# The output projection's second half in a hybrid encoder block: weight parts prepared two tiles ahead on VectorE, the norm spread over the tiles, the first MLP parts cast earlier

## The chip, the cores and the metric

The kernel runs on one core of one Trainium2 chip, as one launch. The metric is device time in microseconds (us), lower is better; a kernel's time is the median of its runs.

## The reference

One encoder layer over 1024 tokens of width 1024, in float32. Cut to what matters here:

```python
def rmsnorm(x, g):
    y = xf * lax.rsqrt(jnp.mean(xf * xf, axis=-1, keepdims=True) + EPS)
    return y * g

def hybrid_mixer(h, ...):
    proj = rmsnorm(h, ln_g) @ w_in          # 1024 x 3104
    ...                                     # 2-D neighbourhood attention (8 heads x 64), gated linear attention (4 heads)
    return jnp.concatenate([y_na, y_gla], axis=-1) @ w_out      # 1024 x 1024

def sqrelu_mlp(h, ln_g, w1, w2):            # w1: 1024 x 4096, w2: 4096 x 1024
    return jnp.square(jax.nn.relu(rmsnorm(h, ln_g) @ w1)) @ w2

h = h + hybrid_mixer(h, ...)
h = h + sqrelu_mlp(h, ...)
out = rmsnorm(h, ln_final_g)
```

## The kernel before

Everything is held transposed: the feature dimension lies on the 128 partitions, the 1024 tokens along the free dimension, in two halves of 512 (`hf` 0 and 1). `hT` is the residual stream, eight tiles `d` of 128 features.

Each float32 operand of a large product is split into two fp32r parts: a high part, which ScalarE makes by a cast (`S.copy`), and a low part, the difference, made by VectorE or GpSimd (POOL in the profile). A product is three matmuls: high times high, high times low, low times high. So every weight tile costs one cast and one subtraction before TensorE can finish with it.

A list scheduler puts the instructions of each engine in a fixed order by priority. Within an engine they then run strictly in that order. `tc.keep_in_program_order` pins an instruction to its place in the program's text among the others pinned so; all of TensorE's instructions are pinned, and so is nearly everything in the MLP (`kp`). `tc.high_priority` moves code ahead.

The part around the change, in order of time:

- Output projection, second half. `sums(1, d, KO, ...)` is 24 matmuls of 128x512 into a PSUM bank `op1_d`, for `d` = 0 to 7; `add` then adds the bank to `hT` on VectorE. Its weights come from `weights(w_out[d], eng)`: a load `wf` (queue of SP), a cast `wh` on ScalarE and one 128x1024 subtraction `wl`, on VectorE for `d` below 4 and on GpSimd from 4 on. `wf`, `wh` and `wl` have two buffers each in the pool `stg`.
- `opl_d` are eight short products that finish the first half of the tokens (the last block of the concatenated heads came late).
- `ff_in(hf, d)` squares `hT[:, d]` on ScalarE (`sq`) and adds it up in `acc0` (GpSimd) or `acc1` (VectorE); `ff_sum(hf)` sums over partitions with a matmul by ones (`v2_0`, `v2_1`), and `rstd_from` makes the reciprocal root from it (`r0`, `r1`) in four ScalarE and two VectorE instructions.
- After tile 2, `r0` is made, and for all eight `k` the normed tile `nf` (VectorE), its cast (ScalarE) and its low part (VectorE): `n0`, the MLP's input for the first half of the tokens.
- The MLP. `First`/`FirstPlain` stages compute `w1` products, `Second`/`SecondPlain` the `w2` ones; four chunks of `w1`/`w2` of 512 KB tiles `A11`, `A12`, `A21`, `A22`. The first chunk is plain: a `FirstPlain` stage of 16 half-steps of 12 matmuls (`u<-...` in the profile; `ph` and `pl` are the high and low part of the weight piece), the first eight for the first half of the tokens (input `n0`), the last eight for the second half (inputs `T4` and `B22`). Then 16 half-steps of `SecondPlain` (`f<-...`).
- Before the `FirstPlain` stage starts, the `ph` and `pl` of its first two half-steps are made (`to_two`); after the first half-step comes `ff_sum(1)`, then `r1`. The normed tiles of the second half (`normed`, `b` in the profile, then a cast and a low part into `T4` or `B22`), and later the sums for a Strassen-like scheme (`sums123`, with GpSimd's `whole`), are given out over the half-steps as `job`s.

`prepare(k)` issues, ahead of half-step `k`, the casts and low parts for half-step `k+2`, the activations of `k-1` and then the jobs.

Of the kernel before, what the change touches and what calls it, by code (L numbers as in the profile page):

```python
# [10 lines left out]
F32 = mybir.dt.float32  # L11
F32R = mybir.dt.float32r
U32 = mybir.dt.uint32
AF = mybir.ActivationFunctionType
ALU = mybir.AluOpType
# [3 lines left out]
P = 128  # L19
D = 1024  # L20
T = 1024
H = 512
NK = D // P
# [43 lines left out]
def block_kernel(ctx, tc, xT, g_mix, w_in, w_z, rpb, na_mask, gu, gb, g_gla, sel_f, sel_b,  # L67
                 rst, w_out, g_ff, w1, w2, g_fin, out):
    nc = tc.nc
    V, S, DMA, G = nc.vector, nc.scalar, nc.sync, nc.gpsimd  # L70

    L = "left"
    R = "right"
    pool = lambda name, side, bufs=1: tc.tile_pool(name=name, bufs=bufs, side=side)
# [7 lines left out]
    stg = stg_stack.enter_context(pool("stg", L, 2))  # L82
# [40 lines left out]
    class Fill:  # L123
# [24 lines left out]
        def run(self, steps=1 << 30):  # L148
            while steps > 0 and self.gens:
                steps -= self.step()  # L150
# [84 lines left out]
    yg_pool = ctx.enter_context(ExitStack())  # L235
# [456 lines left out]
    def to_parts(hf, ks, eng):  # L692
        c = slice(hf * H, (hf + 1) * H)
        t = yhl[hf]
        for k in ks:
            i = KO.index(k)
            S.copy(t[:, i, 0, :], yk(k)[:, c])
            (eng if i % 2 else V).tensor_tensor(t[:, i, 1, :], yk(k)[:, c], t[:, i, 0, :].bitcast(F32), op=ALU.subtract)  # L698
# [5 lines left out]
    def sums(hf, d, ks, eng=None, w=None, ahead=()):  # L704

        w = w or weights(w_out[d], eng)
        o = bank("mm", f"op{hf}_{d}")
        for i, _ in enumerate(out_mm(o, hf, w, ks)):
            to_parts(hf, ahead[i:i + 1], G)
            yield  # L710
        add(hf, d, o)
# [207 lines left out]

    a2 = ctx.enter_context(pool("a2", R))  # L920
    a3 = yg_pool.enter_context(pool("a3", L))
    yp_stack = ExitStack()
    yp = yp_stack.enter_context(pool("op", R, 2))
    n0, acc = half(a2, "n0"), {}

    def ff_in(hf, d):
        c = slice(hf * H, (hf + 1) * H)
        if d == 0:
            acc[hf] = sq = yp.tile([P, H], F32, tag="acc", name=f"acc{hf}")
        else:  # L930
            sq = yp.tile([P, H], F32, tag="sq", name="sq2")
        S.activation(sq, hT[:, d, c], AF.Square)
        if d:
            (V if hf else G).tensor_tensor(acc[hf], acc[hf], sq, op=ALU.add)

# [9 lines left out]
    def to_two(h, l, x, eng=None, kept=False):  # L945

        c = S.copy(h, x)  # L947
        if kept:
            tc.keep_in_program_order(c)
        (eng or V).tensor_tensor(l, x, h.bitcast(F32), op=ALU.subtract)  # L950
# [10 lines left out]
    wk = split(wf, G)  # L961
    to_parts(0, KO[-1:], V)
    to_parts(1, KO, V)
    run(sums(1, 0, KO, w=w10))
    for d in range(NK):
        o = bank(("t", "s", "o")[d % 3], f"opl_{d}")
        t = yhl[0][:, NK - 1]
        run(product(o, wk, lambda k: t[:, 0, :], lambda k: t[:, 1, :], ks=(0,), woff=d * P))
        add(0, d, o)
        ff_in(0, d)  # L970
    ff_in(1, 0)
    for d in range(1, NK):
        run(sums(1, d, KO, V if d < 4 else G))
        ff_in(1, d)
        if d == 2:
            r0 = rstd_from(ff_sum(0), 1.0 / D, yp, "rs", H, "sq", 2, y=acc[0])
            for k in range(NK):
                nf = yp.tile([P, H], F32, tag="nf", name="nf")
                normed_h(nf, 0, k, r0)
                to_two(n0[:, k, 0, :], n0[:, k, 1, :], nf)  # L980
# [215 lines left out]
    class FirstPlain(Stage):  # L1196
# [9 lines left out]
        def mm(self, p, kh):  # L1206
            (hf, m), w = p, self.parts.pop((p, kh))
            if kh == 0:
                self.o = bank("s" if hf else "mm", f"u{hf}_{m}")
            t, k0 = npt[f"B{kh + 1}{hf + 1}"]  # L1210
            for k in range(4):
                for n, (a, x) in enumerate(((w[0], 0), (w[0], 1), (w[1], 0))):
                    PE.matmul(self.o, a[:, k * P:(k + 1) * P], t[:, k0 + k, x, :],
                              start=kh == k == n == 0, stop=kh == 1 and k == 3 and n == 2)
            if kh:
                self.last = self.o
# [59 lines left out]
    def go_on(n):  # L1276
        for _ in range(n):
            k = at[0]
            st, p, i = halves[k]
            prepare(k)  # L1280
            lows = []
            if k + 1 < len(halves) and halves[k + 1][0].gated and halves[k + 1][2] == 0:
                lows = [(halves[n][0], halves[n][1:]) for n in (k + 1, k + 2)]
            if st.gated:
                st.mm(p, i, lows)
            else:
                for t, q in lows:
                    t.lows(*q)
                st.mm(p, i)
            at[0] += 1  # L1290


    f1 = FirstPlain(0)
    stage(f1)
    with tc.high_priority(offset=150):
        for n in range(2):
            p, i = f1.order[n]
            ph = mp.tile([P, H], F32R, tag="ph", name="ph", bufs=3)
            pl = mp.tile([P, H], F32R, tag="pl", name="pl", bufs=3)
            to_two(ph, pl, f1.w.t[f"A{p[1] // 2 + 1}{i + 1}"][:, 0:H])  # L1300
            f1.parts[p, i] = ph, pl
    go_on(1)
    v1 = ff_sum(1)
    r1 = ub("r1")
# [234 lines left out]
```

## Time and profile before

| | |
|---|---|
| median of 3 runs | 1193.68 us (1193.57 to 1195.28) |
| the profiled execution | 1193.91 us, of which the span from first to last instruction is 1192.1 us |
| mean granted TensorE clock | 0.99 |
| busy: TensorE, VectorE, ScalarE, GpSimd | 97%, 73%, 56%, 21% |
| output projection, second half (`op1_1` to `op1_7`) | 493.4 to 537.7 us of the span |
| first MLP stages (`FirstPlain`, `SecondPlain`) | from 539.8 us |

Times in rows of the trace are us from the start of the span. In a timeline row stand the start, the duration, the engine, the source line, the operation, the tile written and the tiles read, the number of merged instructions, and in brackets how long the engine was idle before it and what released it. TensorE's matmuls overlap: a 128x512 one lasts 0.39 us, but the next starts 0.23 us after it, so lost time is read from the distance of starts. A line of the code can be that of a helper: all matmuls are L114, and L1012 and L950 are low parts.

### The profile page before, as it was taken

The page shows a single profiled execution, that of the slowest core. Times are in us where ns is not written, and L with a number is a line of the kernel's source. Part 1 is how long each engine was busy: PE and PEld are TensorE (multiplying, and loading weights), DVE is VectorE, ACT ScalarE, POOL GpSimd, SP SyncE. Part 2 cuts the span into 40 slices and gives each one's busy share as a digit, 9 for nine tenths or more (in the row PEclk, how much of TensorE's full clock was granted, in tenths as well). Part 3 has the DMA queues.
Part 4 walks back from the last instruction along what each step waited for, and adds up shares of the span by engine and source line. Part 5 has one row for each costly group of instructions (what it writes and reads, how often), then busy time and mean ns, then how long its engine had stood idle before and what let it go on. Part 6 is the DMA issues. An engine that isn't in the chain of part 4 may idle for free.

```text
span 1192.1 us, 15428 instructions
## 1 busy us (share of the span) xinstructions
PE 1154.5 (97%) x5632; PEld 945.5 (79%) x5632; DVE 865.0 (73%) x1554; ACT 665.0 (56%) x1222; POOL 248.9 (21%) x203
## 2 busy tenths in 40 slices
PE   8999999989999999999999999999999999999996
PEld 8878778767787878877688888888888888888876
DVE  8777867856767786585858885877859768597455
ACT  6867566556666665435634635545455454453664
POOL 4200000202011124530103230411404114032005
PEclk9999999999999999999999999999999999999999
DMA  7333132322313252330210121111211121111203
GB/s 238 74 87 92 42 73 56 77 65 54 80 42 100 67 177 71 106 106 1 71 66 21 56 71 62 37 54 62 71 53 36 54 71 55 53 53 53 71 1 142
DMA packets 40283, 84.03 MB, mean 70 GB/s; under 512 B 9264, under 2 KB 20656, under 8 KB 40208
## 3 DMA queue, kind: packets, MB, share of 16 engines
q1 hardware_dynamic: 36608, 71.11, 17.8%
q0 software_dynamic: 3456, 11.94, 5.8%
q8 instruction: 44, 0.72, 0.2%
q14 instruction: 31, 0.25, 0.1%
q10 hardware_dynamic: 144, 0.00, 0.0%
HBM read 78.85 MB, written 5.96 MB: 71 GB/s over the span
## 4 chain that ended last, share of the span: by engine, by line
PE 77%; DVE 12%; ACT 6%; issue 2%; DMA 1%; POOL 0%; SPq 0%; DVEq 0%; ACTq 0%
PE f L114 26%; PE u L114 22%; PE proj L114 14%; PE op L114 5%; PE sc L114 2%; PE o L114 2%; PE no L114 2%; PE pt L119 1%; DVE st L595 1%; DVE st L592 1%; DVE pl L1012 1%; DVE asb L587 1%; DVE nf L942 1%; PE sb L114 1%; PE ob L114 1%
## 5 line engine op out<-in xcount | busy, mean ns | idle before, releaser
L1034 ACT CAST ph<-A 128x512 fp32r<-128x512 f32 x166 | 103.0, 621 | 146.4 <-PE f L114 73.6
L1012 POOL TENSOR_TENSOR ul<-uB,uh 128x512 fp32r<-128x512 f32 x84 | 109.2, 1319 | 330.4 <-ACT uh L1047 213.4
L114 PE MATMUL f<-uh,ph 128*128 128x512 f32 x400 | 155.9, 390 | 1.5 <-ACT u L1055 1.3
L114 PE MATMUL f<-ul,ph 128*128 128x512 f32 x400 | 155.7, 389 | 0.1
L114 PE MATMUL f<-uh,pl 128*128 128x512 f32 x400 | 155.7, 389 | 0.0
L1012 DVE TENSOR_TENSOR pl<-A,ph 128x512 fp32r<-128x512 f32 x166 | 112.7, 688 | 52.6 <-ACT ph L1034 52.6
L114 PE MATMUL proj<-nh,wh 128*128 128x512 f32 x352 | 150.5, 428 | 0.0
L114 PE MATMUL proj<-nh,wl 128*128 128x512 f32 x352 | 138.8, 394 | 1.2 <-DMA wl<-in_w_in 1.2
L114 PE MATMUL proj<-nl,wh 128*128 128x512 f32 x352 | 138.3, 393 | 0.0
L1194 DVE TENSOR_TENSOR hT<-hT,f 128x512 f32<-128x512 f32 x168 | 113.0, 686 | 20.0 <-PE f L114 20.0
L114 PE MATMUL u<-n,ph 128*128 128x512 f32 x288 | 90.3, 395 | 2.0 <-ACT ph L947 2.0
L114 PEld LDWEIGHTS f<-uh,ph 128*128 128x128 f32 x400 | 75.1, 188 | 17.9 <-ACT u L1055 1.8
L114 PEld LDWEIGHTS f<-ul,ph 128*128 128x128 f32 x400 | 75.1, 188 | 16.0 <-DVE ul L1012 0.4
L114 PEld LDWEIGHTS f<-uh,pl 128*128 128x128 f32 x400 | 75.1, 188 | 15.6
L114 PEld LDWEIGHTS proj<-nh,wh 128*128 128x128 f32 x352 | 66.6, 189 | 18.1 <-issue 5.6
L1047 ACT CAST uh<-uB 128x512 fp32r<-128x512 f32 x84 | 51.9, 618 | 51.0 <-PE f L114 34.2
L114 PEld LDWEIGHTS proj<-nh,wl 128*128 128x128 f32 x352 | 66.4, 189 | 16.7 <-DMA wl<-in_w_in 1.6
L114 PE MATMUL u<-T,ph 128*128 128x512 f32 x256 | 79.2, 391 | 0.1
L114 PE MATMUL op<-y,wh 128*128 128x512 f32 x240 | 76.9, 401 | 0.4 <-DVE y L698 0.4
L114 PEld LDWEIGHTS proj<-nl,wh 128*128 128x128 f32 x352 | 66.8, 190 | 11.7 <-issue 1.7
L114 PE MATMUL u<-nt,ph 128*128 128x512 f32 x224 | 69.0, 389 | 0.0
L806 ACT ACTIVATE xsc<-xsc,sm 128x384 f32<-128x384 f32 (+1 forms) x64 | 37.3, 584 | 51.4 <-DVE sm L804 51.0
(300 smaller groups left out, 2489.8 us busy)
## 6 DMA issues: line engine op xcount, KB each, us to landing
A<-in_w SPq DMA_DIRECT2D x64, 512.0 KB
wf<-in_w_in SPq DMA_DIRECT2D x22, 512.0 KB
wl<-in_w_in POOLq DMA_DIRECT2D x21, 512.0 KB, 6.8
wf<-in_w_out SPq DMA_DIRECT2D x17, 512.0 KB
hT<-in_xT SPq DMA_DIRECT2D x2, 2048.0 KB
xs<-in_xT SPq DMA_DIRECT2D x6, 512.0 KB
out<-hT SPq DMA_DIRECT2D x4, 512.0 KB
out<-hT SPq DMA_DIRECT2D x8, 256.0 KB
```

The lines of the kernel that those rows point to most:

```text
L114: m = nc.tensor.matmul(*args, **kw)
L119: tc.keep_in_program_order(nc.tensor.transpose(*args, **kw))
L587: V.copy_predicated(asb[hf], sel.bitcast(U32).to_broadcast([P, 4, P]), src.rearrange("p (a b) -> p a b", a=4))
L592: V.scalar_tensor_tensor(st[0:64, i + 1, :], st[0:64, i, :], dec[0:64, i:i + 1], st[0:64, i + 1, :], op0=ALU.mult, op1=ALU.add)
L595: V.scalar_tensor_tensor(st[64:128, j - 1, :], st[64:128, j, :], dec[64:128, j:j + 1], st[64:128, j - 1, :], op0=ALU.mult, op1=ALU.add)
L806: S.activation(x[:, :n], x[:, :n], AF.Exp, scale=-1.0, bias=sm[:, i, 0:1], accum_out=sm[:, i, 1:2])
L942: V.scalar_tensor_tensor(dst, hT[:, d, hf * H:(hf + 1) * H], gff[:, d:d + 1], r, op0=ALU.mult, op1=ALU.mult)
L1012: return kp(eng.tensor_tensor(l, x, h.bitcast(F32), op=ALU.subtract))
L1034: kp(S.copy(ph, x))
L1047: kp(S.copy(uh, x))
L1194: kp(V.tensor_tensor(hT[:, d, c], hT[:, d, c], o[:, s], op=ALU.add))
```

## The change

Four edits.

1. `out_w(d)` replaces `weights` for `d` = 1 to 7 of the second half. It is called two tiles ahead of use (`d` = 1 before `op1_0`, `d` = 2 after it, `d+2` at tile `d`). The parts live in three places: a new pool `w3` for `d` = 1, 4, 7, and the two buffers of `stg` for the others. The subtraction is always on VectorE, in two halves of 128x512, and cast and subtractions are pinned.
2. The norm of the first half of the tokens (`nf`, cast, low part) is spread: two `k` at each of the tiles 3 to 6, rather than all eight after tile 2.
3. The casts of the MLP's first two weight pieces are pinned, and `ff_in(1, 7)`, its square pinned too, now stands after them in the program.
4. `FirstPlain.mm` runs the three kinds of product in the outer loop and `k` in the inner one: four high-high, four high-low, four low-high.

```diff
@@ -919,6 +919,7 @@
 
     a2 = ctx.enter_context(pool("a2", R))
     a3 = yg_pool.enter_context(pool("a3", L))
+    w3 = yg_pool.enter_context(pool("w3", L))
     yp_stack = ExitStack()
     yp = yp_stack.enter_context(pool("op", R, 2))
     n0, acc = half(a2, "n0"), {}
@@ -929,7 +930,9 @@
             acc[hf] = sq = yp.tile([P, H], F32, tag="acc", name=f"acc{hf}")
         else:
             sq = yp.tile([P, H], F32, tag="sq", name="sq2")
-        S.activation(sq, hT[:, d, c], AF.Square)
+        q = S.activation(sq, hT[:, d, c], AF.Square)
+        if hf and d == NK - 1:
+            tc.keep_in_program_order(q)
         if d:
             (V if hf else G).tensor_tensor(acc[hf], acc[hf], sq, op=ALU.add)
 
@@ -961,7 +964,22 @@
     wk = split(wf, G)
     to_parts(0, KO[-1:], V)
     to_parts(1, KO, V)
+
+    def out_w(d):
+
+        wf = stg.tile([P, D], F32, tag="wf", name="wf")
+        DMA.dma_start(wf, w_out[d])
+        places = w3 if d % 3 == 1 else stg
+        wh = places.tile([P, D], F32R, tag="wh", name="wh")
+        wl = places.tile([P, D], F32R, tag="wl", name="wl")
+        tc.keep_in_program_order(S.copy(wh, wf))
+        for c in (slice(0, H), slice(H, D)):
+            tc.keep_in_program_order(V.tensor_tensor(wl[:, c], wf[:, c], wh[:, c].bitcast(F32), op=ALU.subtract))
+        return wh, wl
+
+    w1d = {1: out_w(1)}
     run(sums(1, 0, KO, w=w10))
+    w1d[2] = out_w(2)
     for d in range(NK):
         o = bank(("t", "s", "o")[d % 3], f"opl_{d}")
         t = yhl[0][:, NK - 1]
@@ -970,11 +988,15 @@
         ff_in(0, d)
     ff_in(1, 0)
     for d in range(1, NK):
-        run(sums(1, d, KO, V if d < 4 else G))
-        ff_in(1, d)
+        if d + 2 < NK:
+            w1d[d + 2] = out_w(d + 2)
+        run(sums(1, d, KO, w=w1d.pop(d)))
+        if d < NK - 1:
+            ff_in(1, d)
         if d == 2:
             r0 = rstd_from(ff_sum(0), 1.0 / D, yp, "rs", H, "sq", 2, y=acc[0])
-            for k in range(NK):
+        if 2 < d < NK - 1:
+            for k in (2 * d - 6, 2 * d - 5):
                 nf = yp.tile([P, H], F32, tag="nf", name="nf")
                 normed_h(nf, 0, k, r0)
                 to_two(n0[:, k, 0, :], n0[:, k, 1, :], nf)
@@ -1208,8 +1230,8 @@
             if kh == 0:
                 self.o = bank("s" if hf else "mm", f"u{hf}_{m}")
             t, k0 = npt[f"B{kh + 1}{hf + 1}"]
-            for k in range(4):
-                for n, (a, x) in enumerate(((w[0], 0), (w[0], 1), (w[1], 0))):
+            for n, (a, x) in enumerate(((w[0], 0), (w[0], 1), (w[1], 0))):
+                for k in range(4):
                     PE.matmul(self.o, a[:, k * P:(k + 1) * P], t[:, k0 + k, x, :],
                               start=kh == k == n == 0, stop=kh == 1 and k == 3 and n == 2)
             if kh:
@@ -1297,8 +1319,9 @@
             p, i = f1.order[n]
             ph = mp.tile([P, H], F32R, tag="ph", name="ph", bufs=3)
             pl = mp.tile([P, H], F32R, tag="pl", name="pl", bufs=3)
-            to_two(ph, pl, f1.w.t[f"A{p[1] // 2 + 1}{i + 1}"][:, 0:H])
+            to_two(ph, pl, f1.w.t[f"A{p[1] // 2 + 1}{i + 1}"][:, 0:H], kept=True)
             f1.parts[p, i] = ph, pl
+    ff_in(1, NK - 1)
     go_on(1)
     v1 = ff_sum(1)
     r1 = ub("r1")
```

What this does to the instruction order, at three places. First GpSimd, in the second half of the output projection: `acc0` is the sum of squares of the first half, `wl` are the low parts of tiles 4 to 7, `b11` the first of the MLP's `whole` sums. Before:

```order
L934 TENSOR_TENSOR acc0_4623<-acc0_4623,sq2_4678 128x512
L197 TENSOR_TENSOR wl_4833<-wf_4830,wh_4832 128x1024
L197 TENSOR_TENSOR wl_4868<-wf_4865,wh_4867 128x1024
L197 TENSOR_TENSOR wl_4903<-wf_4900,wh_4902 128x1024
L197 TENSOR_TENSOR wl_4938<-wf_4935,wh_4937 128x1024
L1321 TENSOR_TENSOR b11_5214<-n0_4482 128x512
L1321 TENSOR_TENSOR b11_5261<-n0_4482 128x512
```

After, the four subtractions are gone from GpSimd. VectorE has them instead; from the add of `op1_2` on it now runs (`wl_4785` belongs to tile 5, `wl_4829` to tile 6):

```order
L716 TENSOR_TENSOR hT_4112<-hT_4112,op1_2_4743 128x512
L937 TENSOR_TENSOR acc1_4698<-acc1_4698,sq2_4769 128x512
L230 TENSOR_TENSOR rst_4774<-rst_4774,rsu_4777 128x512
L231 SCALAR_TENSOR_TENSOR acc0_4640<-rst_4774,acc0_4640 128x512
L977 TENSOR_TENSOR wl_4785<-wf_4782,wh_4784 128x512 x2
L945 SCALAR_TENSOR_TENSOR nf_4818<-hT_4112,gff_82,acc0_4640 128x512
L716 TENSOR_TENSOR hT_4112<-hT_4112,op1_3_4789 128x512
L945 SCALAR_TENSOR_TENSOR nf_4822<-hT_4112,gff_82,acc0_4640 128x512
L953 TENSOR_TENSOR n0_4485<-nf_4818,n0_4485 128x512
L937 TENSOR_TENSOR acc1_4698<-acc1_4698,sq2_4815 128x512
L953 TENSOR_TENSOR n0_4485<-nf_4822,n0_4485 128x512
L977 TENSOR_TENSOR wl_4829<-wf_4826,wh_4828 128x512 x2
```

The low part of tile 5 stands before the add of tile 3, that of tile 6 before the add of tile 4, and two normed tiles lie between.

Second, ScalarE where the MLP begins: `sq2` are the squares of tiles 5 to 7, `ph` the first weight pieces. Before:

```order
L932 ACTIVATE sq2_4897<-hT_4112 128x512
L932 ACTIVATE sq2_4932<-hT_4112 128x512
L932 ACTIVATE sq2_4967<-hT_4112 128x512
L947 CAST ph_4992<-A11_4984 128x512
L947 CAST ph_4996<-A12_4986 128x512
```

After:

```order
L933 ACTIVATE sq2_4940<-hT_4112 128x512
L950 CAST ph_5000<-A11_4992 128x512
L950 CAST ph_5004<-A12_4994 128x512
L933 ACTIVATE sq2_5008<-hT_4112 128x512
L1056 CAST ph_5011<-A11_4992 128x512
```

The two casts now stand ahead of the square of tile 7, which waits for the last add. VectorE follows in the same manner; before:

```order
L716 TENSOR_TENSOR hT_4112<-hT_4112,op1_7_4941 128x512
L934 TENSOR_TENSOR acc1_4681<-acc1_4681,sq2_4967 128x512
L950 TENSOR_TENSOR pl_4993<-A11_4984,ph_4992 128x512
L950 TENSOR_TENSOR pl_4997<-A12_4986,ph_4996 128x512
L1012 TENSOR_TENSOR pl_5002<-A11_4984,ph_5000 128x512
```

After, with both `pl` between the last add and the last sum of squares:

```order
L716 TENSOR_TENSOR hT_4112<-hT_4112,op1_7_4951 128x512
L953 TENSOR_TENSOR pl_5001<-A11_4992,ph_5000 128x512
L953 TENSOR_TENSOR pl_5005<-A12_4994,ph_5004 128x512
L937 TENSOR_TENSOR acc1_4698<-acc1_4698,sq2_5008 128x512
L1034 TENSOR_TENSOR pl_5013<-A11_4992,ph_5011 128x512
```

Third, TensorE at the same place, from the first half-step of the MLP to `v2_1`. Before, high-high, high-low and low-high alternate for each `k`:

```order
L114 MATMUL u0_0_5004<-n0_4482,ph_4992 128x512 x2
L114 MATMUL u0_0_5004<-n0_4482,pl_4993 128x512
L114 MATMUL u0_0_5004<-n0_4482,ph_4992 128x512 x2
L114 MATMUL u0_0_5004<-n0_4482,pl_4993 128x512
L114 MATMUL u0_0_5004<-n0_4482,ph_4992 128x512 x2
L114 MATMUL u0_0_5004<-n0_4482,pl_4993 128x512
L114 MATMUL u0_0_5004<-n0_4482,ph_4992 128x512 x2
L114 MATMUL u0_0_5004<-n0_4482,pl_4993 128x512
L114 MATMUL v2_1_5017<-acc1_4681,ones_79 128x512
```

After:

```order
L114 MATMUL u0_0_5015<-n0_4485,ph_5000 128x512 x8
L114 MATMUL u0_0_5015<-n0_4485,pl_5001 128x512 x4
L114 MATMUL v2_1_5028<-acc1_4698,ones_79 128x512
L114 MATMUL u0_0_5015<-n0_4485,ph_5004 128x512 x8
L114 MATMUL u0_0_5015<-n0_4485,pl_5005 128x512 x4
```

The low part `pl` is first read by the ninth matmul of a half-step, not by the third; `v2_1` stays after twelve. The same loop order holds for the half-steps on `T4` and `B22`.

## The prediction

> **What bounds the kernel now.** I read the page's busy shares and chain of waits first, then TensorE's work in stretches of 20 us, then its timeline where a stretch is short of work, and last what the other engines do there.
>
> ```profile
> span 1192.1 us, 15428 instructions
> ...
> PE 1154.5 (97%) x5632; PEld 945.5 (79%) x5632; DVE 865.0 (73%) x1554; ACT 665.0 (56%) x1222; POOL 248.9 (21%) x203
> ...
> PE 77%; DVE 12%; ACT 6%; issue 2%; DMA 1%; POOL 0%; SPq 0%; DVEq 0%; ACTq 0%
> ```
>
> TensorE bounds the kernel: 97% busy, 77% of the chain. Only time in which it stands or runs slowly can be won. The stretches show where (TensorE's busy us with its matmul count come first, the granted clock is third from the end):
>
> ```profile
> 500.00:520.00 20.00, 20.00 (x88) 16.20 (x87) 16.11 (x17) 10.26 (x16) 7.15 (x4) 1.00 0.34 105
> 520.00:540.00 20.00, 15.16 (x57) 11.12 (x56) 14.70 (x17) 7.00 (x12) 7.75 (x4) 0.91 0.21 80
> 540.00:560.00 20.00, 19.91 (x78) 15.63 (x79) 10.75 (x17) 10.63 (x19) 0.00 (x0) 0.91 0.00 0
> ...
> 580.00:600.00 20.00, 17.65 (x73) 13.03 (x72) 17.00 (x26) 13.57 (x25) 1.78 (x1) 1.00 0.24 80
> 600.00:620.00 20.00, 20.00 (x90) 16.57 (x89) 12.23 (x20) 6.99 (x12) 0.00 (x0) 1.00 0.16 52
> ```
>
> A full stretch has 88 to 90 matmuls. From 520 to 560 there are 57 and 78, in tiles 5 to 7 of the projection and the MLP's start, which is where the change works. TensorE's timeline there:
>
> ```profile
> 505.80 0.62 PE L114 MATMUL op<-y,wh 128*128 128x512 f32 x2
> ...
> 521.47 0.61 PE L114 MATMUL op<-y,wh 128*128 128x512 f32 x2
> 523.11 0.50 PE L114 MATMUL op<-y,wl 128*128 128x512 f32 x1 [1.03 <-POOL wl L197]
> ...
> 528.40 0.73 PE L114 MATMUL op<-y,wh 128*128 128x512 f32 x2
> 530.92 0.75 PE L114 MATMUL op<-y,wl 128*128 128x512 f32 x1 [1.79 <-POOL wl L197]
> ...
> 534.67 0.40 PE L114 MATMUL op<-y,wl 128*128 128x512 f32 x1
> ...
> 537.42 0.39 PE L114 MATMUL op<-y,wl 128*128 128x512 f32 x1
> 539.82 0.73 PE L114 MATMUL u<-n,ph 128*128 128x512 f32 x2 [2.01 <-ACT ph L947]
> 540.64 0.50 PE L114 MATMUL u<-n,pl 128*128 128x512 f32 x1
> ...
> 544.58 1.06 PE L114 MATMUL v<-acc,ones 128*128 128x512 f32 x2
> ```
>
> From 505.80 to 521.47 start 69 matmuls: 0.227 us each. That is the measure for what follows. Two kinds of loss show: waits, and after two of them a lower clock:
>
> ```profile
> 532.00:536.00 4.00, 4.00 (x14) 3.17 (x13) 1.58 (x2) 0.63 (x1) 1.79 (x2) 0.70 0.00 0
> 540.00:544.00 4.00, 3.91 (x11) 2.81 (x12) 1.79 (x3) 0.81 (x2) 0.00 (x0) 0.65 0.00 0
> 260.00:264.00 4.00, 3.25 (x8) 1.59 (x9) 2.73 (x14) 2.20 (x7) 0.00 (x0) 0.67 0.64 176
> 596.00:600.00 4.00, 3.60 (x16) 2.98 (x17) 2.63 (x5) 2.61 (x6) 0.00 (x0) 1.00 0.41 135
> ...
> 260.37 0.44 PE L114 MATMUL sc<-k00p,q 128*128 128x384 f32 x1 [2.21 <-DVE sm L804]
> ...
> 596.39 0.50 PE L114 MATMUL f<-uh,ph 128*128 128x512 f32 x1 [1.35 <-ACT u L1055]
> ```
>
> Waits of 1.79, 2.01 and 2.21 us were followed by clocks of 0.70, 0.65 and 0.67; the wait of 1.35 was not (1.00).
>
> **The change part by part.** *Weights two tiles ahead.* In tiles 6 and 7 the low part comes late, since GpSimd needs 2.4 us for it and starts only after a cast that itself waits its turn:
>
> ```profile
> 520.67 2.38 POOL L197 TENSOR_TENSOR wl<-wf,wh 128x1024 fp32r<-128x1024 f32 x1 [4.70 <-ACT wh L196]
> 528.42 2.44 POOL L197 TENSOR_TENSOR wl<-wf,wh 128x1024 fp32r<-128x1024 f32 x1 [5.36 <-ACT wh L196]
> 530.82 2.97 POOL L1321 TENSOR_TENSOR b<-n 128x512 f32<-128x512 f32 x2
> ...
> 513.75 2.77 DVE L942 SCALAR_TENSOR_TENSOR nf<-hT,gff,acc 128x512 f32<-128x512 f32 x1
> ...
> 516.44 0.68 DVE L950 TENSOR_TENSOR n<-nf,n 128x512 fp32r<-128x512 f32 x1
> 517.04 0.68 DVE L934 TENSOR_TENSOR acc<-acc,sq 128x512 f32<-128x512 f32 x1
> ...
> 518.25 1.40 DVE L942 SCALAR_TENSOR_TENSOR nf<-hT,gff,acc 128x512 f32<-128x512 f32 x2
> ...
> 516.38 85.84 SPq L1021 DMA_DIRECT2D A<-in_w  x10
> ```
>
> Lost in tile 6: 523.11 less 521.47 less two starts (0.45) is 1.2, and 0.1 in the next starts. Tile 7: 530.92 less 528.40 less 0.45 is 2.1, 0.2 ahead of it, and the slow clock from 530.92 to 534.67, nine matmuls in 3.75 instead of 2.04, is 1.7. Together 5.3, of which 1.7 is the clock's.
>
> Does it all go? VectorE now carries per tile two half subtractions, two `nf`, two low parts, an add and a sum of squares. Its starts lie 0.60 apart (516.44, 517.04), 0.70 for `nf` (two in 1.40): 6 x 0.60 + 2 x 0.70 = 5.0 us against a tile's 24 x 0.227 = 5.45. It is nearly full, but the 128x1024 subtraction on GpSimd also goes, beside which one `nf` took 2.77 instead of 0.70; that is 2 us back per tile. Two of GpSimd's `whole` sums stay (2.97 for both). Walking down the two orders with these durations, tile 6's low part is done near 516 for a need at 521, tile 7's near 521 (523 with both `whole` sums in its way) for a need at 526.5. With margins of 3.5 to 5 us I take all 5.3.
>
> Both ends of that: if no two VectorE instructions overlapped (8 x 0.69 = 5.5 per tile, 0.1 over the tile's 5.45) and both `whole` sums stood fully in its way (3.0), it would be 3.3 us late after four tiles, of which the 3.0 are in the 523 already: no loss in the weights. So the cost lies between 0 and what that lag does at the MLP's start, below. A gain beyond 5.3 is excluded, since the waits and the slow stretch are all there is to win here.
>
> The loads: SP issued `A11` at 516.38, behind tile 7's weights, which waited for GpSimd's low part of tile 5. Now that is VectorE's, right behind `r0`, near 511; the MLP's pieces come no later. Cost 0.
>
> *Norm spread.* The same 24 instructions, off TensorE's path; they fill tiles 3 to 6 instead of 511 to 528. `n0` is complete near 527, the MLP needs it near 532. Cost 0; gone if VectorE lags 5 us.
>
> *MLP parts sooner.* Before, the casts stood behind the square of tile 7 and so behind the last add:
>
> ```profile
> 537.85 0.69 DVE L716 TENSOR_TENSOR hT<-hT,op 128x512 f32<-128x512 f32 x1 [3.51 <-PE op L114]
> ...
> 539.17 1.12 ACT L947 CAST ph<-A 128x512 fp32r<-128x512 f32 x2
> ...
> 539.29 0.69 DVE L934 TENSOR_TENSOR acc<-acc,sq 128x512 f32<-128x512 f32 x1 [0.76 <-ACT sq L932]
> ...
> 545.67 0.69 ACT L221 ACTIVATE rst<-v,small 128x512 f32<-128x512 f32 x1 [4.86 <-PE v L114]
> ...
> 551.57 0.62 ACT L1325 CAST T<-b 128x512 fp32r<-128x512 f32 x1 [1.16 <-DVE b L1336]
> ...
> 568.91 1.30 POOL L1321 TENSOR_TENSOR b<-n 128x512 f32<-128x512 f32 x1 [35.12 <-DVE b L1336]
> ...
> 595.75 0.59 ACT L1055 ACTIVATE u<-u 128x512 f32<-128x512 f32 x1
> ```
>
> Call E the moment at which the first MLP matmul could start, 537.42 + 0.23 = 537.65 before. `v2_1` started at 544.58, 6.93 after E; twelve matmuls need 2.73. The rest is the wait (2.17), one for `pl` (0.36) and a slow clock (1.67).
>
> After: the casts are done ahead of E. On VectorE the add starts 0.2 after E (537.85), `pl` ends at 0.2 + 0.60 + 0.69 = 1.5, and the ninth matmul, the first to read it, stands at 8 x 0.227 = 1.8: no wait. The second `pl` and the sum of squares follow 0.60 apart, so `acc1` is ready at 0.2 + 3 x 0.60 + 0.69 = 2.7, where `v2_1` stands: at most 0.1 late. So `v2_1` starts 2.8 after E: 4.1 won. With the lag of 3.3 above, less the 2.8 us that VectorE is idle ahead of this add in my walk, it would be 0.5 less.
>
> *Loop order.* In the first eight half-steps it gives `pl` six more matmuls of time. Against that, the tenth half-step (`B22`) now reads the last normed tile's high part at its fourth matmul and its low part at its eighth, before at its tenth and eleventh. So I expect about 1.5 to 2 us of waiting there, where before there was 0.4. It costs nothing at the end, for this reason: from `v2_1` on, ScalarE and VectorE work off one chain, `r1`, then a normed tile, its cast, its low part, by turns (551.57 waits for VectorE's `b`, and so on), up to the activation at 595.75, for which TensorE waits 1.35 us at 596.39. The chain's instructions and order stay the same, so 596.39 moves with `v2_1`, whatever TensorE waits before; a slow clock of 1.7 us on the way would eat the 1.35 and leave 0.4 to pay. After 600 TensorE is full and unchanged.
>
> The sum: 5.3 + 4.1 = 9.4 us off the profiled execution of 1193.91 (span 1192.1 plus 1.8): 1184.5. The runs' median is 0.2 lower, which I leave out.
>
> [...]
>
> **The rivals.** A: the MLP's start still waits, because VectorE comes to the last add late or the pinned casts come late. The weights' 5.3 stay won, of the 4.1 about half: 1186 to 1188. For it speaks VectorE's 5.0 of 5.45 us; against it, its 2.8 idle us ahead of that add.
>
> B: the slow clock stays where it is, for a cause of its own, or strikes at the longer wait on `B22`: 1.7 us per spell, so 1186.2 with one, 1187.9 with both. Against it: each slow stretch quoted stands right behind a long wait.
>
> C, the change doesn't do what it says: on ScalarE the casts of tiles 5 to 7 stay behind `r0`'s four instructions and the squares, so the low parts are again just in time, now on a fuller VectorE: the 9.4 would shrink to under 2.4, 1192 to 1194. Against it: the cast of tile 5 stands right behind `r0`, 5 us ahead of tile 4's end.
>
> D, slower: the SP queue. Tile 7's weights, and `A11` behind them, wait for VectorE's low part of tile 5, which waits for `r0`. The one load of this size with a landing time, on another queue, takes 6.8 us:
>
> ```profile
> wl<-in_w_in POOLq DMA_DIRECT2D x21, 512.0 KB, 6.8
> ```
>
> With 1.1 for the cast (539.17: two of 512 columns in 1.12) and 1.3 for the low part (0.60 + 0.69), tile 7 could start 9.2 us after that issue, and `v2_1` 5.45 + 2.8 later. If tile 5's low part came at 527 instead of 511, `v2_1` would be where it was, and each us beyond costs one: 3 us beyond gives 1197. Nothing in the rows holds `r0` so long.
>
> **How the numbers follow.** Forecast 0.70, A 0.12, B 0.09, C 0.05, D 0.04. A measurement of this kernel tells 0.2% (2.4 us) from no change. Forecast, A and B are faster: 0.91. C lies mostly within: 0.05. D is slower: 0.04. The range: 0.5 from VectorE's lag and 0.4 from a slow spell at `B22` on the upper side, then A and B up to 1188; on the lower side the chain from `v2_1` can shorten where a `whole` sum on GpSimd (568.91, 1.30 us) no longer meets a VectorE instruction: 1.5 at most, 1183.0.
>
> **What would show it.** Right: no wait for `wl` in the projection, granted clock 1.00 from 500 to 545, `v2_1` near 535.2 instead of 544.58, more waiting at `u<-B`, the activation of 595.75 near 586.4. Wrong: TensorE waiting for `acc` at `v2_1` or for `pl` (A), a clock under 1 without a wait (B), VectorE's starts over 5.45 us of work per tile (C), `ph` waiting for a load (D).

## The result and the profile after

| | before | after |
|---|---|---|
| median | 1193.62 us (6 runs) | 1185.88 us (6 runs), ratio 0.9933 [0.992, 0.9946] |
| measured again beside later kernels | 1194.03 us (9 runs) | 1185.22 us (5 runs), ratio 0.9926 [0.9914, 0.9939] |
| profiled execution | 1193.91 us | 1185.78 us |

The change wins 7.7 us in the first comparison and 8.8 in the second; the forecast was 9.4, to 1184.5. The page of the changed kernel, its busy shares and chain, and below them TensorE's work in stretches of 20 us:

```profile
span 1183.9 us, 15432 instructions
PE 1150.3 (97%) x5632; PEld 944.6 (80%) x5632; DVE 862.6 (73%) x1565; ACT 665.3 (56%) x1222; POOL 241.7 (20%) x199
PE 82%; DVE 9%; ACT 6%; issue 1%; DMA 1%; SPq 0%; DVEq 0%; ACTq 0%
520.00:540.00 20.00, 20.00 (x88) 15.93 (x87) 15.96 (x25) 11.10 (x19) 1.67 (x1) 1.00 0.06 24
540.00:560.00 20.00, 19.86 (x88) 15.99 (x86) 15.09 (x24) 11.28 (x20) 0.00 (x0) 1.00 0.00 1
560.00:580.00 20.00, 18.84 (x81) 14.77 (x80) 16.99 (x25) 12.39 (x22) 3.06 (x2) 1.00 0.27 81
580.00:600.00 20.00, 17.87 (x76) 13.83 (x76) 12.98 (x21) 11.53 (x22) 0.00 (x0) 1.00 0.22 77
```

The stretches from 520 to 560, which had 57 and 78 matmuls, have 88 each, at a clock of 1.00. What is left to win stands from 560 to 600.

TensorE's timeline gives points that both kernels pass. `v<-acc` is first `v2_0`, then `v2_1`; `vf` is the last matmul group of the kernel. Before:

```profile
504.24 1.02 PE L114 MATMUL v<-acc,ones 128*128 128x512 f32 x2
1181.99 1.13 PE L114 MATMUL vf<-fsq,ones 128*128 128x256 f32 x4 [0.84 <-DVE fsq L1442]
```

After:

```profile
505.36 1.02 PE L114 MATMUL v<-acc,ones 128*128 128x512 f32 x2
505.81 1.03 PE L114 MATMUL op<-y,wh 128*128 128x512 f32 x2
533.46 2.08 PE L114 MATMUL u<-n,ph 128*128 128x512 f32 x8
536.28 1.06 PE L114 MATMUL v<-acc,ones 128*128 128x512 f32 x2
561.31 1.83 PE L114 MATMUL u<-B,ph 128*128 128x512 f32 x5 [1.04 <-ACT B L1348]
588.22 0.50 PE L114 MATMUL f<-uh,ph 128*128 128x512 f32 x1 [1.33 <-ACT u L1077]
1173.73 1.13 PE L114 MATMUL vf<-fsq,ones 128*128 128x256 f32 x4 [0.85 <-DVE fsq L1465]
```

From `v2_0` to the last group it is 677.75 us before and 668.37 after: 9.38 less. But `v2_0` itself stands 1.12 us later. That arises near 265 us, far ahead of the first changed instruction: the matmul that starts at 260.37 before stands 0.27 us earlier in the changed kernel, the one at 272.58 stands 1.08 us later. So the profiles differ by 8.2 us of span, not 9.4. Measured from `v2_0`, the two parts of the stretch can be compared over all kernels below, without what happens ahead of it:

| kernel | median us against that of before beside it | `v2_0` at | `v2_0` to `v2_1` | `v2_1` to last group |
|---|---|---|---|---|
| before | | 504.24 | 40.34 | 637.41 |
| after | -7.74 | 505.36 | 30.92 | 637.45 |
| after, again | -8.81 | 505.93 | 30.85 | 637.60 |
| weights and norm alone | -4.85 | 505.53 | 35.07 | 637.48 |
| start of the MLP alone | -3.54 | 506.00 | 36.17 | 637.47 |
| after, old loop order | -7.02 | 506.07 | 32.05 | 637.44 |
| after, casts late | -4.23 | 506.00 | 34.73 | 637.49 |
| the same, wait filled | -6.41 | 504.36 | 33.13 | 637.49 |
| after, lows on GpSimd | -0.88 | 503.96 | 38.93 | 637.49 |
| after, one tile ahead | -7.42 | 504.06 | 32.30 | 637.58 |
| after, norm at once | +3.59 | 504.18 | 43.68 | 637.60 |
| after, old order on T4/B22 | -7.48 | 507.96 | 30.86 | 637.59 |
| after, norm one ahead | -13.15 | 505.68 | 30.85 | 631.99 |
| before, norm one ahead | -5.26 | 504.26 | 38.83 | 632.02 |

The last column is 637.4 to 637.6 in all rows but the last two: whatever moves `v2_1` there moves the end by as much.

### The profile page after: what moved, and what is told of

It is laid out like the page before. It is cut to its first block, busy times and chain, and to the rows that moved or that the text cites. A ratio compares the mean times of both kernels' runs of the same rounds, so it can differ in the third digit from the quotient of the medians.

```text
span 1183.9 us, 15432 instructions
## 1 busy us (share of the span) xinstructions
PE 1150.3 (97%) x5632; PEld 944.6 (80%) x5632; DVE 862.6 (73%) x1565; ACT 665.3 (56%) x1222; POOL 241.7 (20%) x199
## 4 chain that ended last, share of the span: by engine, by line
PE 82%; DVE 9%; ACT 6%; issue 1%; DMA 1%; SPq 0%; DVEq 0%; ACTq 0%
PE f L114 26%; PE u L114 23%; PE proj L114 14%; PE op L114 7%; PE sc L114 2%; PE o L114 2%; PE no L114 2%; PE pt L119 1%; PE sb L114 1%; DVE st L595 1%; DVE st L592 1%; PE ob L114 1%; DVE asb L587 1%; PE z L114 1%; DMA wl<-in_w_in 1%
## 5 line engine op out<-in xcount | busy, mean ns | idle before, releaser
L114 PE MATMUL u<-n,ph 128*128 128x512 f32 x288 | 85.3, 391 | 0.0
```

The lines of the kernel that those rows point to most:

```text
L114: m = nc.tensor.matmul(*args, **kw)
```

## The experiments

### Halves of the change

Edits 1 and 2 alone, that is the changed kernel with

```diff
-            for n, (a, x) in enumerate(((w[0], 0), (w[0], 1), (w[1], 0))):
-                for k in range(4):
+            for k in range(4):
+                for n, (a, x) in enumerate(((w[0], 0), (w[0], 1), (w[1], 0))):
...
-            to_two(ph, pl, f1.w.t[f"A{p[1] // 2 + 1}{i + 1}"][:, 0:H], kept=True)
+            to_two(ph, pl, f1.w.t[f"A{p[1] // 2 + 1}{i + 1}"][:, 0:H])
...
-    ff_in(1, NK - 1)
```

and `ff_in(1, 7)` back behind `sums(1, 7)`, its square not pinned.

> The change's edits 1 and 2 alone (weights ahead with lows on VectorE, norm spread); casts of the first MLP pieces and the loop order as before. Theory: the stretch from the first matmul of op1_3 to E (the moment the first MLP matmul could start) keeps its shortening, 33.0 to 27.7 us, no waits for wl, clock 1.00 from 500 to E. The MLP's start keeps its wait of about 2 us, the wait for pl and the slow clock behind it: E to v2_1 about 6.9 us. Together 5.3 us off the time before. Rival (the slow clock in the projection has its own cause): 1.7 us of slow running stay between 500 and E, only 3.6 won. Second rival (the slow spell at the MLP's start comes from the one in the projection, not from the wait): E to v2_1 about 5.2 and 7.0 won.

Edits 3 and 4 alone are the same lines the other way round, on the kernel before.

> The kernel before with edits 3 and 4 alone (casts of the first MLP pieces ahead of the last square, loop order). Theory: the waits of 1.0 and 1.8 us for wl and the slow clock behind the second stay (33.0 us from op1_3 to E); E to v2_1 falls from 6.9 to about 2.8 and the end follows v2_1: 4.1 us off the time before. If the two halves of the change are independent, this and the weights-and-norm kernel add to the change's gain, 9.3 by the stretches of its profile. Rival (they need each other, since VectorE or ScalarE comes late to the start of the MLP when the weights are late): E to v2_1 above 4 us and under 3 won.

TensorE's timeline and one stretch of 4 us, first with edits 1 and 2 alone, then with 3 and 4 alone:

```profile
535.80 0.74 PE L114 MATMUL u<-n,ph 128*128 128x512 f32 x2 [2.01 <-ACT ph L948]
536.00:540.00 4.00, 3.92 (x11) 2.75 (x11) 1.77 (x3) 0.79 (x2) 0.00 (x0) 0.64 0.00 0
```

```profile
532.68 0.51 PE L114 MATMUL op<-y,wl 128*128 128x512 f32 x1 [1.79 <-POOL wl L197]
539.42 0.84 PE L114 MATMUL u<-n,ph 128*128 128x512 f32 x3
532.00:536.00 4.00, 3.32 (x9) 2.62 (x10) 3.24 (x3) 1.66 (x3) 3.56 (x3) 0.63 0.00 0
```

Each half removes its own waits and leaves those of the other: 40.34 less 35.07 is 5.27, 40.34 less 36.17 is 4.17, together 9.44 against the 9.42 of the whole change. The halves are independent, and the three rivals, two on the clock and one on mutual need, fall.

### Which edit at the MLP's start

The loop order alone undone (the first two lines of the diff above):

> The changed kernel with the old loop order (k outermost) in every plain half-step. Theory: pl is read by the third matmul, 0.45 us after E, but VectorE has it only about 1.5 us after E, so v2_1 stands about 3.9 us after E instead of 2.8, and the end follows: 1.0 us slower than the changed kernel. At B22 the wait of 1.04 us mostly vanishes, which is worth nothing, because the wait at the gate activation (1.33 us) takes it up. Rival (what TensorE loses at B22 counts in full): the 1.0 lost at the start is won back there, no difference.

The casts alone late again (the rest of that diff):

> The changed kernel without edit 3: the casts of the first MLP pieces stand behind the last square again, the loop order stays new. Theory: TensorE waits about 2.0 to 2.2 us for ph at E, the granted clock falls behind that wait as it did in the kernel before (1.7 us), pl is no longer waited for: v2_1 about 6.5 us after E instead of 2.8, the end 3.7 us later than in the changed kernel. Rival (the wait costs only itself): v2_1 about 4.9 after E, 2.1 us later.

```profile
535.72 0.50 PE L114 MATMUL u<-n,pl 128*128 128x512 f32 x1 [0.92 <-DVE pl L953]
```

That was the old loop order: the wait for `pl` costs 1.1 us ahead of `v2_1` (32.05 for 30.9), and the shorter wait at `B22` (0.44 us instead of 1.04) brings nothing back. With late casts:

```profile
536.28 3.06 PE L114 MATMUL u<-n,ph 128*128 128x512 f32 x8 [2.01 <-ACT ph L948]
536.00:540.00 4.00, 3.72 (x11) 2.93 (x12) 2.25 (x4) 1.27 (x3) 0.00 (x0) 0.65 0.00 0
```

34.73 for 30.9: 3.8 us, as expected, of which 2.17 are the wait in distances of starts and the rest the clock. The early cast is worth more than the loop order, but the order has a share of its own.

### Does the wait at B22 cost anything?

```diff
-            for n, (a, x) in enumerate(((w[0], 0), (w[0], 1), (w[1], 0))):
-                for k in range(4):
-                    PE.matmul(...)
+            steps = [(n, k) for n in range(3) for k in range(4)]
+            if hf:
+                steps = [(n, k) for k in range(4) for n in range(3)]
+            for n, k in steps:
+                a, x = ((w[0], 0), (w[0], 1), (w[1], 0))[n]
+                PE.matmul(...)
```

> The changed kernel with the new loop order in the half-steps on the first half of the tokens alone; those on T4 and B22 go k outermost again. Theory (the chain of ScalarE and VectorE from v2_1 sets the gate activation): v2_1 stays 2.8 us after E, the wait of 1.04 us at B22 falls to about 0.4, but from v2_1 to the matmul behind the gate activation it stays 51.9 us: no difference to the changed kernel, within 0.3 us. Rival (TensorE's own waits add up): 51.9 becomes 51.0 to 51.3 and the kernel is 0.6 to 0.9 us faster.

```profile
565.25 0.50 PE L114 MATMUL u<-B,ph 128*128 128x512 f32 x1 [0.42 <-DVE B L1034]
590.84 0.50 PE L114 MATMUL f<-uh,ph 128*128 128x512 f32 x1 [1.35 <-ACT u L1077]
```

The wait at `u<-B` falls from 1.04 to 0.42 us; from `v2_1` (538.82) to the gate matmul it is 52.02, in the changed kernel 51.94. No difference: TensorE is not the bound there.

### What the chain from v2_1 is worth

VectorE makes the normed tile `n+1` before the low part of tile `n`:

```diff
     def normed(key, k):
+        n = 4 * (key == "B22") + k
+        if n == 0:
+            norm_b(0)
+        if n < 7:
+            norm_b(n + 1)
+        put(key, k, b[key, k])
+
+    def norm_b(n):
+        key, k = ("B12", "B22")[n // 4], n % 4
...
-        put(key, k, t)
```

> The changed kernel with the second half's normed tiles one ahead: VectorE makes the normed tile n+1 before the low part of tile n, so that ScalarE's cast of n+1 need not wait for it. Theory (the chain from v2_1 is ScalarE and VectorE by turns, and sets the gate activation): each of eight links loses about 0.6 us of waiting; what can be won is what TensorE still waits between v2_1 and 600 us, 1.04 at B22, 0.69 and 1.33 at the activations, 3.1 us in all: 2 to 3 us faster than the changed kernel, v2_1 to the gate matmul 49 to 50 us instead of 51.9. Rival (the engines' summed work, not the turns, fills these 52 us): no difference within 0.3 us.

The three stretches of 20 us with this edit on the changed kernel:

```profile
540.00:560.00 20.00, 20.00 (x90) 16.57 (x89) 18.30 (x29) 14.71 (x27) 2.81 (x1) 1.00 0.05 12
560.00:580.00 20.00, 20.00 (x90) 16.58 (x89) 17.68 (x27) 12.56 (x22) 1.79 (x1) 1.00 0.28 94
580.00:600.00 20.00, 20.00 (x90) 16.48 (x89) 13.11 (x22) 9.62 (x17) 0.00 (x0) 1.00 0.16 54
```

All stretches are full (90 matmuls each, against 88, 81 and 76), and from `v2_1` to the last group it is 5.5 us less. The chain theory holds and its rival falls, but the size was missed: I expected 2 to 3 us and the gate matmul 49 to 50 us behind `v2_1`; it stands 46.54 behind it, 5.4 less than the 51.94 of the changed kernel. I had summed the waits in brackets, 3.1. Each wait costs 0.16 more by the distance of starts (0.39 for the last matmul ahead of it instead of 0.23), the next start comes another 0.11 late, and there are short stops without a bracket. At a median of 1180.88 us, ratio 0.9888 [0.9875, 0.9902], this is the fastest version: 4.3 us ahead of the changed kernel on the same chip, by the medians of four and five runs.

The same edit on the kernel before:

> The kernel before with nothing but the second half's normed tiles one ahead, as in the run on the changed kernel that won 5.5 us from v2_1 to the last matmul. Theory (the stretch from v2_1 on is bound by the turns of ScalarE and VectorE in the kernel before too, apart from what stands ahead of v2_1): v2_1 where it was (40.3 us after v2_0), from v2_1 to the last matmul 632 instead of 637.4 us: 5.4 us faster than the kernel before. Rival (the norm ahead pays only with the new loop order, which has B22 needed sooner): 2 us or less.

From `v2_1` it saves 5.4 us, as expected. It also showed something else, which is told below with the clock.

### What makes the weights early: the engine, the distance or the spread

The low parts on GpSimd, still two tiles ahead:

```diff
-        for c in (slice(0, H), slice(H, D)):
-            tc.keep_in_program_order(V.tensor_tensor(wl[:, c], wf[:, c], wh[:, c].bitcast(F32), op=ALU.subtract))
+        tc.keep_in_program_order(G.tensor_tensor(wl, wf, wh.bitcast(F32), op=ALU.subtract))
```

> The changed kernel with the low parts of the second half's weights on GpSimd, one 128x1024 subtraction each, still two tiles ahead. Theory (being two tiles ahead is what wins, and the engine is free): GpSimd needs 2.4 us of each tile's 5.45, so no wait for wl in the projection, E to v2_1 about 2.8: within 1 us of the changed kernel. Rival (VectorE is what wins): on GpSimd the sums of squares acc0 stand in the same queue, and each 128x1024 subtraction holds up VectorE's nf by about 2 us; VectorE comes late to the last add and the MLP's start waits 1 to 3 us: slower than the changed kernel by 2 to 5 us.

TensorE's two waits, then VectorE beside GpSimd's subtractions, of which the one from 521.87 is shown (the one before it runs from 515.99 to 518.38):

```profile
522.93 0.70 PE L114 MATMUL op<-y,wh 128*128 128x512 f32 x2 [1.52 <-DVE hT L716]
531.76 1.19 PE L114 MATMUL op<-y,wh 128*128 128x512 f32 x2 [3.13 <-DVE hT L716]
516.03 2.90 DVE L945 SCALAR_TENSOR_TENSOR nf<-hT,gff,acc 128x512 f32<-128x512 f32 x1
521.87 2.56 POOL L976 TENSOR_TENSOR wl<-wf,wh 128x1024 fp32r<-128x1024 f32 x1 [3.49 <-ACT wh L975]
522.10 0.68 DVE L716 TENSOR_TENSOR hT<-hT,op 128x512 f32<-128x512 f32 x1
522.70 2.28 DVE L945 SCALAR_TENSOR_TENSOR nf<-hT,gff,acc 128x512 f32<-128x512 f32 x1
```

No wait for `wl` at all, and yet 8.0 of the 9.4 us are gone, by waits that neither theory named: for `hT`, that is for VectorE's add, which frees the PSUM bank that tile `d+2` needs. From 531.00 to 537.81 the granted clock is 0.50, and the slow matmuls behind the second wait make up nearly 3 of the 8.0. VectorE's `nf` takes 2.90 and 2.28 instead of 0.70 while a subtraction runs; the add, which reads one operand from PSUM, stays at 0.68 beside it. The long `nf` at 516.03 makes the add at 522.10 late. Ahead of the second wait stand the one at 522.70 and then two VectorE instructions of 1.77 us each instead of 0.68 beside the two `whole` sums (524.39 to 527.83), which GpSimd runs straight behind its last subtraction.

One tile ahead instead of two:

```diff
-    w1d[2] = out_w(2)
...
-        if d + 2 < NK:
-            w1d[d + 2] = out_w(d + 2)
+        if d + 1 < NK:
+            w1d[d + 1] = out_w(d + 1)
```

> The changed kernel with the weights' parts made one tile ahead instead of two, still on VectorE, the norm still spread. Tile 7's low part then stands behind the add of tile 5: its first half done near 527, its second near 529, for needs at 527.8 and 529.6. Theory (VectorE in place of GpSimd is what wins in the projection, and the second tile ahead buys only margin): no wait for wl above 0.3 us, within 0.5 us of the changed kernel. Rival (two tiles ahead is what wins): waits for wl of 1 to 2 us in tiles 6 and 7 with a slow clock behind, 2 to 4 us slower.

```profile
523.03 0.50 PE L114 MATMUL op<-y,wl 128*128 128x512 f32 x1 [0.82 <-DVE wl L977]
```

Neither theory is right: `v2_1` stands 32.30 us after `v2_0` instead of 30.9. Most of these 1.4 us is one wait in tile 6 (not 7), with no slow clock behind it (1.00 from 523 to 545). So on VectorE and with the norm spread, one tile ahead already brings about three quarters of the 5.3, and the second tile the rest.

The norm of all eight `k` after tile 2 again:

```diff
-        if 2 < d < NK - 1:
-            for k in (2 * d - 6, 2 * d - 5):
+        if d == 2:
+            for k in range(NK):
```

> The changed kernel with the norm of the first half made for all eight k after tile 2 again, rather than two at each of the tiles 3 to 6; the weights stay as changed. On VectorE the low parts of tiles 5 to 7 then stand behind all eight nf, all eight low parts of n0, and the adds of tiles 3 and 4: 8 x 0.70 + 8 x 0.60 + 4 x 0.60 = 12.8 us from 511.8 on, so tile 5's low part is done near 526 for a need near 517. Theory (the spread, which the prediction booked at nothing, is what lets the weights come early): TensorE waits 8 to 9 us in tile 5 for wl, runs slowly for some 2 us behind that wait, and waits no more at the MLP's start: 9 to 11 us slower than the changed kernel, slower than the kernel before by 1 to 3. Rival (ScalarE and VectorE work off the norm fast enough): at most 2 us slower than the changed kernel.

```profile
525.70 1.22 PE L114 MATMUL op<-y,wh 128*128 128x512 f32 x2 [9.58 <-ACT wh L975]
523.42 1.28 ACT L950 CAST n<-nf 128x512 fp32r<-128x512 f32 x2 [1.85 <-DVE nf L945]
524.61 1.99 ACT L975 CAST wh<-wf 128x1024 fp32r<-128x1024 f32 x2
528.00:532.00 4.00, 4.00 (x12) 3.08 (x11) 0.55 (x2) 1.05 (x1) 0.00 (x0) 0.56 0.94 330
```

12.8 us worse than the changed kernel, and slower than the kernel before (ratio 1.0031 [1.0019, 1.0044]). The wait is 9.58 us, and what ends it is not the subtraction but the cast ahead of it: ScalarE, too, ran its list in order, the casts of `n0` from 523.42 and `wh` behind them from 524.61, and the casts of `n0` waited for VectorE's `nf` (1.85 us in the first row of ScalarE). I had expected 9 to 11 in all; the wait is longer than the 8 to 9 that I named, and the slow clock lasts longer than I allowed for (0.50 until 531.52, 5.8 us after the wait).

### The clock: is it the standing still?

The kernel with late casts, with nine matmuls of data already there put into its wait:

```diff
+    fl = bank("o", "fill")
+    for _ in range(9):
+        PE.matmul(fl, n0[:, 0, 0, 0:P], n0[:, 0, 0, :], start=True, stop=True)
     go_on(1)
```

> The kernel with the late casts and the new loop order (whose first MLP matmul waited 2.01 us and was followed by a slow clock, v2_1 34.73 us after v2_0), with nine more 128x512 matmuls of data that are there already, into a bank that nothing reads, put into that wait (9 x 0.227 = 2.0 us). Theory (it is TensorE's standing still that is followed by the lower clock): the clock stays at 1.00, v2_1 33.0 to 33.2 us after v2_0, the kernel 1.6 us faster than without the nine, though it does more. Rival (the lower clock comes from something else at this place, such as the change of stage or of weights): the clock falls to about 0.65 all the same and v2_1 stays at 34.7.

```profile
532.46 2.20 PE L114 MATMUL fill<-n 128*128 128x512 f32 x9
534.64 2.11 PE L114 MATMUL u<-n,ph 128*128 128x512 f32 x8
536.00:540.00 4.00, 4.00 (x18) 2.94 (x17) 0.61 (x2) 1.45 (x3) 0.00 (x0) 1.00 0.00 0
```

The first MLP matmul still has to wait for `ph` and TensorE does more, and `v2_1` comes 1.60 us sooner (33.13 for 34.73), at a clock of 1.00. Between these two profiles the slow clock goes with TensorE's standing still. But it does not always follow. The kernel before with the norm one ahead is the same as the kernel before up to `v2_1`, and has the same waits of 1.79 and 2.01 us; its first slow spell begins in the first row:

```profile
531.50:532.00 0.50, 0.50 (x3) 0.41 (x2) 0.50 (x1) 0.00 (x0) 0.50 (x1) 0.58 0.00 0
539.86 0.73 PE L114 MATMUL u<-n,ph 128*128 128x512 f32 x2 [2.01 <-ACT ph L947]
540.00:544.00 4.00, 3.91 (x15) 2.57 (x16) 1.83 (x4) 0.85 (x2) 0.00 (x0) 1.00 0.00 0
```

Here the clock stays at 1.00 behind the wait of 2.01, and `v2_1` stands 38.83 us after `v2_0` instead of 40.34. In the kernel before, in stretches of half a us at the edges of its two slow spells:

```profile
531.00:531.50 0.50, 0.50 (x2) 0.40 (x3) 0.50 (x2) 0.00 (x0) 0.50 (x1) 0.50 0.00 0
534.00:534.50 0.50, 0.50 (x3) 0.39 (x2) 0.34 (x1) 0.00 (x0) 0.00 (x0) 0.59 0.00 0
541.00:541.50 0.50, 0.50 (x3) 0.46 (x2) 0.50 (x2) 0.00 (x0) 0.00 (x0) 0.74 0.00 0
544.50:545.00 0.50, 0.50 (x2) 0.23 (x1) 0.00 (x0) 0.00 (x0) 0.00 (x0) 0.85 0.00 0
```

Inside the spells the granted clock is 0.50 (first row). A clock of 0.59 in half a us is then 0.41 us at 0.50 and 0.09 at 1.00, and by these four rows (an estimate from them) the spells run from 531.0 to 534.41 and from 541.24 to 544.65, 3.41 us each. The first begins 0.1 us after its wait of 1.79 ends (530.92), the second 1.4 us after its wait of 2.01 (539.82). The wait of 1.52 us with the lows on GpSimd had none behind it (1.00 from 523 to 530.5). Why one wait of 2.01 us is followed by a spell and another is not, no run isolates.

That leaves a rival for the run with the nine matmuls, too: its spell might have stayed away without them. One profile of it can't exclude that, and the medians, 2.2 us apart (-4.23 and -6.41), hold what lies ahead of `v2_0` as well. What was measured agrees with the theory: 33.13 us at a clock of 1.00, for a forecast of 33.0 to 33.2.

The slow spells ahead of the change also bear on the shortfall against the forecast of 1184.5. With the changed kernel run again:

> The changed kernel once more, for the 1.1 us by which its profile was late already at the first matmul of v2_0, in code that the change does not touch. Theory (chance: the length of a slow-clock stretch near 265 us differs from one execution to the next): v2_0 starts anywhere from 504.0 to 506.1 us here too, from v2_0 to the last matmul it is 668.4 us within 0.2 again, and the median stays within 1 us of 1185.9. Rival (the change itself makes the part ahead longer): v2_0 at 505.4 or later again, and no execution below 1184.7.

`v2_0` to the last group is 668.45 us, as it was (668.37), and the median 1185.22. But `v2_0` stood at 505.93 and the fastest execution took 1184.71, which the rival named as its sign too, so this run alone decides nothing. The others do: the kernel with the filled wait, the same as the changed kernel up to tile 7, has `v2_0` at 504.36, and the kernels that change nothing ahead of it have it at 506.00 and 504.26. Over all kernels it stands from 503.96 to 507.96. One place where this comes from, a stretch of 2 us not long behind a wait of 2.2 us that ends near 260 in both; before, then after:

```profile
266.00:268.00 2.00, 2.00 (x11) 1.37 (x9) 1.04 (x3) 0.00 (x0) 0.00 (x0) 1.00 0.04 8
```

```profile
266.00:268.00 2.00, 2.00 (x8) 1.59 (x7) 0.00 (x0) 0.00 (x0) 0.00 (x0) 0.70 0.00 0
```

The slow spell there is over by 266 in one profile and not in the other, for the same code: by stretches of half a us it lasts 3.41 us, from 261.35 to 264.76, against 6.82 us, from 260.38 to 267.20 (granted clock 0.50 inside both).

## Why the prediction was right

- Weights two tiles ahead: 5.3 us forecast. From the start of `op1_3` to the first possible MLP matmul it is 504.69 to 537.65 before and 505.81 to 533.46 after, 5.31 less; alone, 5.27. The margins held: tile 7's low part was done at 525.11 and first read at 528.48.
- The MLP's start: 4.1 forecast. 6.93 before, 536.28 less 533.46 = 2.82 after, 4.11 less; alone, 4.17. `v2_1` was forecast at 535.2, and stands 1.1 later because `v2_0` does.
- The wait that moves to `B22` and costs nothing: forecast 1.5 to 2; the row has 1.04, in distances of starts with a second stop at 562.63 it is 1.7. That it is free is shown by the kernel with the old order on `T4` and `B22`. From `v2_1` to the gate matmul it was 51.81 and is 51.94.
- The sum: 9.4 forecast, 9.38 from `v2_0` to the last group, and 1.12 lost ahead of it, where the slow spells lie differently. The medians' 7.7 and 8.8 lie below. The 3.4 us that I booked for slow spells are not there in every execution: the kernel before with the norm one ahead, the same up to `v2_1`, had only one of the two (38.83 for 40.34), and the granted clock of the kernel before goes from 0.987 to 0.993 over 35 executions beside the later kernels. Taken as lost time, one minus the clock times the span is 11.2 us in the mean of these and 8.6 in that of eleven executions of the changed kernel, so the mean gain by the clock is about 2.5 us instead of 3.4 (an estimate: the clock has three digits, and which spells were missing is known for the profiled executions alone). Treating them as certain was the one term of the sum that was too large; the sum fits its own profile so well because that profile has both spells. Rival B, that the clock has its own cause, was half right: where the waits went the spells went (1.00 from 520 to 560), but a wait of 2.01 us had a spell behind it in one profile and none in another.
- The slow spells went with their waits: with edits 1 and 2 alone the wait of 2.01 us stays and with it a clock of 0.64, with edits 3 and 4 alone the wait of 1.79 us and 0.63. That the same wait can also pass at 1.00 is what the prediction lacked.
- Too confident: the 2.8 us "that VectorE is idle ahead of this add in my walk". The timelines of VectorE and ScalarE in the changed kernel:

```profile
531.46 0.68 DVE L716 TENSOR_TENSOR hT<-hT,op 128x512 f32<-128x512 f32 x1
532.90 0.69 DVE L937 TENSOR_TENSOR acc<-acc,sq 128x512 f32<-128x512 f32 x1 [0.76 <-ACT sq L933]
533.66 0.69 DVE L716 TENSOR_TENSOR hT<-hT,op 128x512 f32<-128x512 f32 x1
532.24 0.63 ACT L933 ACTIVATE sq<-hT 128x512 f32<-128x512 f32 x1 [1.42 <-DVE hT L716]
532.77 1.13 ACT L950 CAST ph<-A 128x512 fp32r<-128x512 f32 x2
```

  The add of tile 6 starts at 531.46, though that tile's last matmul ended at 528.19: VectorE was 3.3 us late, as much as the upper end that the prediction had worked out. The last add starts right behind the sum of squares of tile 6, with no idle time, and the first cast, the first of the two in 1.13 us, ends about 533.4, at the very moment when TensorE needs it (533.46). Beside the two `whole` sums on GpSimd (from 516.92 and 521.68) an `nf` took 1.78 us instead of 0.75, which used up part of the margin; where all of it went is not worked out here. That TensorE did not wait for this cast was luck by 0.1 us, and rival A was nearer than its 0.12.
- Norm spread: "cost 0" was right as a cost, but it is not a side matter. Without it the change loses 12.8 us; it is what lets edit 1 work while VectorE and ScalarE go through their lists in order (`wh` at 524.61 behind the casts of `n0`), and the prediction did not see that.

## What to carry to other kernels

Sum lost time by the distances of starts, not by the waits in brackets, and add separately what a slow clock may take behind a wait (1.7 us here for a spell of 3.41), as a chance and not as a certainty. When work moves to another engine, ask which of that engine's other instructions a third party waits for: here GpSimd's subtraction held up VectorE's norm (`nf` 2.90 us instead of 0.70), and through it the PSUM bank, so the engine (8.0 us) mattered more than the distance ahead (1.4 us). Where two engines work a chain by turns, issue the next link's first half before the last half of this one: that took 5.5 us, without any work less.

## What the runs showed of the hardware

Slow spells of TensorE had a granted clock of 0.50. They lasted 3.41 us twice in the stretch of the kernel before (from 531.0 and 541.24), 6.82 us near 260 in the changed kernel, 6.8 with the lows on GpSimd (531.00 to 537.81) and 10.2 with the norm at once (521.28 to 531.52). One of 3.41 us cost 1.7 us: nine matmuls in 3.75 us instead of 2.04. After the wait of 9.58 us the clock stayed at 0.50 until 531.52, 5.8 us after TensorE had begun again. The length does not follow the wait alone: near 260, behind 2.21 us in the kernel before, the spell lasted 3.41 us, behind 2.20 us in the changed kernel 6.82, and in the changed kernel with the norm one ahead one of 6.83 us lies there too (260.98 to 267.81).

How much standing brings a slow spell is not settled. In tile 7, 1.79 us were followed by one in three runs; at the MLP's start, 2.01 us were followed by one in three runs and not in a fourth. In the run with the start of the MLP alone a single wait of 1.34 us, ahead of 64x128 matmuls, was followed by a spell from 232.67 to 236.08:

```profile
231.02 1.13 PE L114 MATMUL a<-qD,kI 64*128 64x128 f32 x14 [1.34 <-DVE asb L587]
232.00:236.00 4.00, 4.00 (x12) 3.10 (x11) 3.79 (x7) 1.56 (x2) 3.06 (x4) 0.58 0.72 210
```

In the kernel before the same wait of 1.34 us ends at 230.95, and the clock is 1.00 from 229 to 236. So the time of standing alone does not decide; what else does, no run here isolates.
